# Hybrid FoX/mLSTM/PEER block on one core: the second token block's key searches spread among its own products, and one staging buffer for the first half of the gate table

## The chip, the core and the metric

One Trainium2 chip, one of its cores. The program runs once per execution; the metric is the device time of that execution in microseconds (us). TensorE is called PE, VectorE DVE, ScalarE ACT, GpSimd POOL and SyncE SP, as in the profile. DVE, ACT, PE, POOL and SP each work through a queue of their own in order; a wait at the head of a queue holds back all that stands behind it there.

## The reference, cut to what matters

The layer is a mixer (attention and mLSTM heads) followed by PEER, a lookup in a table of 16384 one-neuron experts. The change lies in PEER alone:

```python
q = (h @ w_query).reshape(B, S, PEER_HEADS, PEER_QDIM)      # 256 tokens, 8 heads x 256
s1 = einsum('bshd,nd->bshn', q[..., :half], sub_keys_1)     # 128 keys
s2 = einsum('bshd,nd->bshn', q[..., half:], sub_keys_2)
v1, i1 = top_k(s1, 16);  v2, i2 = top_k(s2, 16)
cand = (v1[..., :, None] + v2[..., None, :])                # 256 sums
vs, pos = top_k(cand, 16)
idx = i1[pos // 16] * 128 + i2[pos % 16]                    # 16 experts of a head
g = softmax(vs)
a = gelu(einsum('td,thkd->thk', x, expert_down[idx]))       # 2048 wide
out = einsum('thk,thkd->td', g * a, expert_up[idx])
```

## The kernel before, in words

The 256 tokens are two blocks of 128 (`t` = 0, 1), one token to a partition. After the mixer, the PEER part has four pieces.

*Search.* `head(t, h)` finds the 16 experts of head h for block t: `keys` and `chosen` are some 35 small DVE instructions that read the scores from `later[t]` and write `idx[t]` (in the order below `idx_4976` is block 0, `idx_4977` block 1). 16 searches in all.

*Gather and products.* The rows of `expert_down` are fetched by indirect DMA on POOL's queue, one DMA for one expert slot k of all 128 tokens: 128 rows of 2048 floats, 1 MB, into a tile `rows`. `issue()` fetches as many as there are free buffers. The buffers are those of the tags in the list `homes`, two to a tag, taken in turn: eight with `raw`, `rawb`, `hi`, `lo`, six without `lo`. `dot()` takes the oldest one: a DVE instruction multiplies the tile by the token's `ht[t]` and sums into `dots[t]`; then its buffer is free. 128 products to a block. `ready` holds the slots that are found and not yet fetched, block 0 first; `waiting(t)` counts those of block t.

*Gates as a table.* When block t's searches are over, `softmax(t)` runs on DVE with an Exp on ACT in between (DVE's next step, the sum into `gs`, waits for it). When its 128 products are over, `turned(t, [2])` makes the weights. Then the weights are scattered into a table (one column for each expert) with PE: for 16 tokens at a time, `first_ones(tb)` builds 16 one-hot matrices `o1` and `gates(tb)` the weighted `o2`, PE multiplies them, `out_of_psum()` copies the results on ACT to the tile `stage` (12 of 16 column groups) and to `kept` (the other 4), in four pieces of 4 tokens; after the fourth, SP sends `stage` to DRAM (`gd<-stage`, 768 KB, in pieces of 512 bytes). `tb` 0 to 7 are the first half of the table (block 0; `o1` and `o2` built on ACT), 8 to 15 the second (`o2` on DVE). `out_of_psum` runs behind: the last two pieces of `tb` are copied after the first `o2` of `gates(tb + 1)`.

*Up projection.* `expert_up` is multiplied by the table on PE (the long last stage), with the last 512 columns done by a second gather, `rows<-in_upr`.

Before, the order written out by hand is: six of block 0's searches alternate with three of block 1's, 14 to 16 products of block 0 between; then block 0's softmax and its last 26 products; then block 1's searches 4 to 7, four products after each, `gates(0)` in between; `softmax(1)`; then 112 products, and with them `gates(1)` to `gates(7)`. `later[0]`, `later[1]`, `stage` and the loaded `g` share the tag `q`, which has two buffers in turn. All the instructions of this part are issued through one helper, so their line in the profile is L69.

Of the kernel before, what the change touches and what calls it, by code (L numbers as in the profile page):

```python
# [7 lines left out]
F32 = mybir.dt.float32  # L8
# [10 lines left out]
P = 128  # L19
D = 2048  # L20
KD = D // P
T = 256
NT = T // P
# [10 lines left out]
PEER_H = 8  # L34
# [46 lines left out]
def hybrid_block(ctx: ExitStack, tc: tile.TileContext, x, c, wada, cst, shp, wst, wg, wmv, wfv,  # L81
# [485 lines left out]
    todo = {i: [] for i in range(24)}  # L567
# [28 lines left out]
    for b in range(KD):  # L596
        o = gemm_p(wout[b], lambda k: cath[k // 8][:, k % 8], lambda k: catl[k // 8][:, k % 8])
        g = mod[:, GATE1 * KD + b:GATE1 * KD + b + 1]
# [61 lines left out]
    pg = ctx.enter_context(tc.tile_pool(name="pg", bufs=2))  # L660
# [42 lines left out]

    slots = pk.tile([P, TOPK], BF16, bufs=1, name="slots")
    nc.scalar.activation(slots, iota[:, 0:TOPK], AF.Copy)
    later = [pg.tile([P, PEER_H, 2, P], F32, tag="q", name="later") for _ in range(NT)]
    sp = [None]

    def query(u):
# [50 lines left out]
    ready, flight = [], []  # L760
# [14 lines left out]
    def dot(n=1):  # L775

        for _ in range(n):
            if not flight:
                return
            _, t, k, u = flight.pop(0)  # L780
            nc.vector.scalar_tensor_tensor(u, u, 1.0, ht[t], op0=ALU.mult, op1=ALU.mult,
                                           accum_out=dots[t][:, k:k + 1])
            issue()

    def softmax(t):
        g = ev[t][:, 2]
        nc.vector.tensor_tensor(g, vs[t], vs[t][:, :, 0:1].to_broadcast([P, PEER_H, TOPK]), op=ALU.subtract)
        nc.scalar.activation(g, g, AF.Exp)
        gs = pk.tile([P, PEER_H], F32, tag="gs", name="gs")
        nc.vector.reduce_sum(gs, g, axis=AX.X)  # L790
        nc.vector.reciprocal(gs, gs)
        nc.vector.tensor_tensor(g, g, gs[:, :, None].to_broadcast([P, PEER_H, TOPK]), op=ALU.mult)

    def turned(t, parts):

        if 2 in parts:
            w = flat(ev[t][:, 2], 0, PEER_H)
            nc.scalar.activation(dots[t], dots[t], AF.Gelu)
            nc.vector.tensor_tensor(w, w, dots[t], op=ALU.mult)
        ep = bank([P, len(parts), P], "at")  # L800
        for i, p in enumerate(parts):
            nc.tensor.transpose(ep[:, i], flat(ev[t][:, p], 0, PEER_H), ident)
        nc.scalar.activation(est[t][:, parts[0]:parts[-1] + 1], ep, AF.Copy)


    TB = 16
# [6 lines left out]
    def first_ones(tb, engine=None):  # L813

        half, t0 = divmod(tb * TB, P)
        if 2 * HB - 4 <= tb < 2 * HB - 2:
            o1 = px.tile([P, TB, P], F32, name="o1")
        else:
            o1 = (ring, pg)[tb % 2].tile([P, TB, P], F32, tag=("lo", "o1")[tb % 2], name="o1", bufs=2)
        if engine is None:  # L820
            for tl in range(TB):
                t = t0 + tl
                nc.scalar.activation(o1[:, tl], iota, AF.Abs, bias=est[half][:, 0, t:t + 1], scale=-1.0)
            nc.scalar.activation(o1, o1, AF.Relu, scale=-1.0, bias=one)
        else:
            engine.tensor_tensor(o1, iota[:, None, :].to_broadcast([P, TB, P]),
                                 est[half][:, 0, t0:t0 + TB, None].to_broadcast([P, TB, P]), op=ALU.is_equal)
        ones_at[tb] = o1

    def gates(tb):  # L830
        if not kept:
            kept.append(const.tile([P, GK, T, 8], F32, tag="hs", name="kept"))
        stage = pg.tile([P, 16 - GK, TB, 8], F32, tag="q", name="stage")
        ts = slice(tb * TB, (tb + 1) * TB)
        half, t0 = divmod(tb * TB, P)
        col = est[half]
        o1 = ones_at.pop(tb)
        for t8 in range(0, TB, 8):

            o2 = pg.tile([P, 8, P], F32, tag="o2", name="o2")  # L840
            for tl in range(8):
                t = t0 + t8 + tl
                if half:
                    nc.vector.tensor_scalar(o2[:, tl], iota, col[:, 1, t:t + 1], col[:, 2, t:t + 1],
                                            op0=ALU.is_equal, op1=ALU.mult)
                else:
                    nc.scalar.activation(o2[:, tl], iota, AF.Abs, bias=col[:, 1, t:t + 1], scale=-1.0)
            if not half:
                nc.scalar.activation(o2, o2, AF.Relu, scale=-1.0, bias=one)
                for tl in range(8):  # L850
                    t = t0 + t8 + tl
                    nc.scalar.activation(o2[:, tl], o2[:, tl], AF.Copy, scale=col[:, 2, t:t + 1])
                out_of_psum()
            for t4 in range(0, 8, 4):
                gp = bank([P, 4, P], "at")
                for i in range(4):
                    nc.tensor.matmul(gp[:, i], o1[:, t8 + t4 + i], o2[:, t4 + i], start=True, stop=True)
                full.append((gp, stage, tb, t8 + t4))
            if half:
                out_of_psum()  # L860
# [14 lines left out]
    def head_scores(h):  # L875
        qs = [query(2 * h)]
        qs.append(query(2 * h + 1))
        scores(2 * h, qs[0])
        if h == 0:
            for j in range(4):  # L880
                by_tokens(0, j)
        scores(2 * h + 1, qs[1])

    def head(t, h):
        keys(h, t, later[t][:, h])
        chosen(t, h, h + 1)
        issue()

    def waiting(t):
        return sum(r[0] == t for r in ready)  # L890

    head_scores(0)
    head(0, 0)
    head_scores(1)
# [3 lines left out]
    for j in range(4):  # L898
        by_tokens(1, j)
    head_scores(3)  # L900
    behind = [(0, 1), (0, 2), (1, 1), (0, 3), (0, 4), (1, 2), (0, 5), (0, 6), (1, 3), (0, 7)]
    for i, (t, h) in enumerate(behind):
        while t == 0 and waiting(0) > 2:
            dot()
        head(t, h)
        if i < 2:
            head_scores(4 + 2 * i)
            head_scores(5 + 2 * i)
        if i == 1:
            homes[:] = ["raw", "rawb", "hi", "lo"]  # L910
    softmax(0)
    turned(0, [0, 1])
    while flight[0][1] == 0:
        dot()
        if sum(f[1] == 0 for f in flight) + waiting(0) == 8:
            homes[:] = ["raw", "rawb", "hi"]
    turned(0, [2])
    for tb in (0, 1):
        first_ones(tb)
    head(1, 4)  # L920
    dot(4)
    gates(0)
    first_ones(2)
    head(1, 5)
    dot(4)
    first_ones(3)
    for h in (6, 7):
        head(1, h)
        dot(4)
    softmax(1)  # L930
    turned(1, [0, 1])
    pk_cm.__exit__(None, None, None)
    px_cm = tc.tile_pool(name="px", bufs=2)
    px = px_cm.__enter__()
    todo = len(flight) + len(ready) - 12
    for tb in range(1, HB):
        dot(todo // (HB - 1))
        gates(tb)
        first_ones(tb + 3)
    out_of_psum()  # L940
    for tb in range(HB + 3, HB + 6):
        first_ones(tb)


# [74 lines left out]

    def group(g):  # L1020
        if GK <= g < 16:
            gt[g] = pg.tile([P, T, 8], F32, tag="q", name="g")
            nc.sync.dma_start(gt[g], gd[g])

    def gated(b):
# [149 lines left out]
```

## Time and profile before

| | |
|---|---|
| time, median of 3 (lowest to highest) | 1948.27 us (1943.56 to 1955.91) |
| the profiled execution | 1948.02 us; span from the first to the last instruction 1946.3 us |
| busy, share of the span | PE 65%, DVE 87%, ACT 42%, POOL 45% |
| mean DMA rate | 341 GB/s |

The profiled execution stands 0.25 us under the median. The page gives the busy time of each engine over the whole span; the program has stages with different limits, so the shares of single stretches are what is read below. A dot's busy time on DVE reads 2.29 us, but dots that follow each other without a wait start 2.21 us apart: neighbours overlap by some 0.08 us, and a wait reads that much too short.

### The profile page before, as it was taken

The page shows a single profiled execution, that of the slowest core. Times are in us where ns is not written, and L with a number is a line of the kernel's source. Part 1 is how long each engine was busy: PE and PEld are TensorE (multiplying, and loading weights), DVE is VectorE, ACT ScalarE, POOL GpSimd, SP SyncE. Part 2 cuts the span into 40 slices and gives each one's busy share as a digit, 9 for nine tenths or more (in the row PEclk, how much of TensorE's full clock was granted, in tenths as well). Part 3 has the DMA queues.
Part 4 walks back from the last instruction along what each step waited for, and adds up shares of the span by engine and source line. Part 5 has one row for each costly group of instructions (what it writes and reads, how often), then busy time and mean ns, then how long its engine had stood idle before and what let it go on. Part 6 is the DMA issues. An engine that isn't in the chain of part 4 may idle for free. (4 is left out here: it accounts for less than half of the span.)

```text
span 1946.3 us, 24456 instructions
## 1 busy us (share of the span) xinstructions
PE 1271.7 (65%) x9078; PEld 1191.5 (61%) x9078; DVE 1685.3 (87%) x2383; ACT 813.5 (42%) x1324; POOL 869.7 (45%) x516
## 2 busy tenths in 40 slices
PE   5899999999999900000011322102699999999998
PEld 3899977798988700000011222102699999999998
DVE  7887898897787799999999888888788898888885
ACT  4332374584421000000074776801555555555552
POOL 0000000000004366666755888883167777677760
PEclk9999999999999955555555555555799999999999
DMA  9977767787869979797977999998699999999992
GB/s 396 369 317 289 286 258 294 290 335 285 314 238 422 420 293 421 318 382 320 371 305 282 421 421 421 421 423 352 194 369 354 347 386 371 375 372 386 364 359 100
DMA packets 126649, 663.71 MB, mean 341 GB/s; under 512 B 13377, under 2 KB 38337, under 8 KB 55745
## 3 DMA queue, kind: packets, MB, share of 16 engines
q1 hardware_dynamic: 69186, 326.58, 43.9%
q0 software_dynamic: 57344, 335.58, 42.6%
q8 instruction: 71, 1.16, 0.2%
q14 instruction: 48, 0.39, 0.0%
HBM read 647.42 MB, written 14.68 MB: 340 GB/s over the span
## 5 line engine op out<-in xcount | busy, mean ns | idle before, releaser
L69 POOL DMA_INDIRECT rows<-in_down,idx x256 | 513.9, 2007 | 822.8 <-DVE tk L69 582.4
L69 DVE SCALAR_TENSOR_TENSOR rows<-rows,ht 128x2048 f32<-128x2048 f32 x256 | 577.6, 2290 | 60.0 <-DMA rows<-in_down,idx 58.7
L69 POOL DMA_INDIRECT rows<-in_upr,idx x256 | 355.6, 1389 | 202.3 <-DVE acc L69 87.0
L69 PE MATMUL ps<-w,whi 128*128 128x256 f32 x2048 | 353.9, 278 | 9.5 <-ACT w L69 8.8
L69 PEld LDWEIGHTS ps<-w,whi 128*128 128x128 f32 x2048 | 310.8, 189 | 10.0 <-ACT w L69 9.0
L69 PE MATMUL at<-sh,e 128*128 128x128 f32 x6 | 2.2, 437 | 452.0 <-DVE e L69 452.0
L69 PE MATMUL ps<-w,wlo 128*128 128x256 f32 x1024 | 284.1, 277 | 0.0
L69 PEld LDWEIGHTS at<-sh,e 128*128 128x128 f32 x6 | 0.9, 197 | 453.0 <-issue 453.0
L69 PE MATMUL at<-o,o 128*128 128x128 f32 x512 | 95.7, 368 | 161.6 <-ACT o L69 153.2
L69 PEld LDWEIGHTS ps<-w,wlo 128*128 128x128 f32 x1024 | 193.4, 189 | 0.0
L69 PEld LDWEIGHTS at<-o,o 128*128 128x128 f32 x512 | 90.3, 272 | 167.3 <-ACT o L69 157.9
L69 DVE SCALAR_TENSOR_TENSOR acc<-rows,e,acc 128x512 f32<-128x512 f32 x254 | 189.4, 746 | 1.6
L69 PE MATMUL at<-w,wht 128*128 128x256 f32 x1536 | 189.5, 283 | 0.0
L69 PEld LDWEIGHTS at<-w,wht 128*128 128x128 f32 x1536 | 186.4, 192 | 0.0
L69 DVE TENSOR_TENSOR wlo<-raw,whi 128x1024 fp32r<-128x1024 f32 x128 | 155.6, 1219 | 25.0 <-ACT whi L69 20.0
L69 ACT ACTIVATE whi<-raw 128x1024 fp32r<-128x1024 f32 x128 | 128.6, 1053 | 116.2 <-PE ps L69 71.0
L113 ACT ACTIVATE whi<-raw 128x2048 fp32r<-128x2048 f32 x65 | 124.1, 1911 | 117.6 <-PE ps L347 28.1
L114 DVE TENSOR_TENSOR wlo<-raw,whi 128x2048 fp32r<-128x2048 f32 x65 | 148.4, 2286 | 24.9 <-ACT whi L113 24.7
L69 PE MATMUL ps<-hf,raw 128*128 128x256 f32 x512 | 115.1, 385 | 6.5 <-DMA raw<-in_wq 5.4
L69 ACT ACTIVATE wht<-raw 128x1024 fp32r<-128x1024 f32 x64 | 64.4, 1054 | 116.0 <-PE at L69 104.8
L69 ACT ACTIVATE e<-e 128x128 f32<-128x128 f32 x2 | 0.6, 309 | 267.8 <-DVE e L69 267.8
L69 PEld LDWEIGHTS ps<-hf,raw 128*128 128x128 f32 x512 | 97.3, 192 | 22.4 <-DMA raw<-in_wq 8.1
(248 smaller groups left out, 2858.4 us busy)
## 6 DMA issues: line engine op xcount, KB each, us to landing
raw<-in_up SPq DMA_DIRECT2D x96, 1024.0 KB
raw<-in_wada SPq DMA_DIRECT2D x45, 1024.0 KB
early<-in_wada SPq DMA_DIRECT2D x44, 1024.0 KB
raw<-in_wst SPq DMA_DIRECT2D x32, 1024.0 KB
raw<-in_wout SPq DMA_DIRECT2D x16, 1024.0 KB
raw<-in_wq SPq DMA_DIRECT2D x16, 1024.0 KB
gd<-stage SPq DMA_DIRECT2D x16, 768.0 KB
g<-gd SPq DMA_DIRECT2D x12, 1024.0 KB
```

Source lines behind the costliest of these rows:

```text
L69: return self.tc.keep_in_program_order(f(*args, **kwargs))
L113: nc.scalar.activation(hi, raw, AF.Copy)
L114: nc.vector.tensor_tensor(lo, raw, hi.bitcast(F32), op=ALU.subtract)
```

## The change

Block 1's searches no longer stand between block 0's. All of block 0's searches come first, then each of block 1's is placed as soon as at most 8 of block 1's found slots are still unfetched. A new function, `first_half`, is called after each product: once block 0's last product is done, it issues the whole first half of the table (`gates(0)` to `gates(7)`) in one go. `later[1]` stays in use longer, so the tag `q` is split into `q0` and `q1` with one buffer each, and the first half's `stage` uses `q0` alone. The second half's `stage` and the loaded `g` alternate between the two.

```diff
-    later = [pg.tile([P, PEER_H, 2, P], F32, tag="q", name="later") for _ in range(NT)]
+    later = [pg.tile([P, PEER_H, 2, P], F32, tag=f"q{t}", name="later", bufs=1) for t in range(NT)]
...
-        stage = pg.tile([P, 16 - GK, TB, 8], F32, tag="q", name="stage")
+        stage = pg.tile([P, 16 - GK, TB, 8], F32, tag=f"q{tb % 2 if tb >= HB else 0}", name="stage", bufs=1)
...
+    halves = [-1]
+
+    def first_half():
+
+        of_first = sum(f[1] == 0 for f in flight) + waiting(0)
+        if halves[0] == 0 and of_first == 8:
+            homes[:] = ["raw", "rawb", "hi"]
+            halves[0] = 1
+        if halves[0] == 1 and of_first == 0:
+            halves[0] = 2
+            turned(0, [2])
+            for tb in range(4):
+                first_ones(tb)
+            for tb in range(HB):
+                gates(tb)
+                if tb + 4 < HB:
+                    first_ones(tb + 4)
+            out_of_psum()
...
-    behind = [(0, 1), (0, 2), (1, 1), (0, 3), (0, 4), (1, 2), (0, 5), (0, 6), (1, 3), (0, 7)]
+    behind = [(t, h) for t in range(NT) for h in range(1, PEER_H)]
     for i, (t, h) in enumerate(behind):
-        while t == 0 and waiting(0) > 2:
+        while waiting(t) > (2, 8)[t] or (t and waiting(0)):
             dot()
+            first_half()
         head(t, h)
...
-    while flight[0][1] == 0:
-        dot()
-        if sum(f[1] == 0 for f in flight) + waiting(0) == 8:
-            homes[:] = ["raw", "rawb", "hi"]
-    turned(0, [2])
-    for tb in (0, 1):
-        first_ones(tb)
-    head(1, 4)
-    dot(4)
-    gates(0)
-    first_ones(2)
...
+        if (t, h) == (0, PEER_H - 1):
+            halves[0] = 0
+            softmax(0)
+            turned(0, [0, 1])
     softmax(1)
     turned(1, [0, 1])
...
-    todo = len(flight) + len(ready) - 12
-    for tb in range(1, HB):
-        dot(todo // (HB - 1))
-        gates(tb)
-        first_ones(tb + 3)
-    out_of_psum()
-    for tb in range(HB + 3, HB + 6):
+    for tb in range(HB, HB + 6):
         first_ones(tb)
...
-            gt[g] = pg.tile([P, T, 8], F32, tag="q", name="g")
+            gt[g] = pg.tile([P, T, 8], F32, tag=f"q{g % 2}", name="g", bufs=1)
```

On DVE, at the first of the three places where a search of block 1 stood between block 0's: the end of that search, and the products behind it.

```order
-L69 TENSOR_TENSOR lk<-ab,slots 128x512
-L69 TENSOR_TENSOR lk<-lk,ki_4963 128x512
-L69 TENSOR_REDUCE e_4975<-lk 128x2x16
-L69 SCALAR_TENSOR_TENSOR idx_4977<-e_4975 128x16
 L69 SCALAR_TENSOR_TENSOR rows,dots_4978<-rows,ht_4960 128x2048 x14
 L69 MAX kv<-later 128x8
```

The 14 products (`dots_4978` is block 0's) now follow straight on block 0's search (0, 2); the searches (1, 1), (1, 2) and (1, 3) have gone from here.

On DVE, behind the search (1, 4) of before, the end of a search of block 1 and the products up to the next one.

```order
 L69 TENSOR_REDUCE e_4975<-lk 128x2x16
 L69 SCALAR_TENSOR_TENSOR idx_4977<-e_4975 128x16
-L69 SCALAR_TENSOR_TENSOR rows,dots_4979<-rows,ht_4961 128x2048 x4
+L69 SCALAR_TENSOR_TENSOR rows,dots_4979<-rows,ht_4961 128x2048 x16
 L69 MAX kv<-later 128x8
```

Where 4 products of block 1 (`dots_4979`) stood between two searches, there are 16. In full, DVE's order behind the search (0, 2) is now 14 products, then four times a search with 16 products, search (0, 7) with softmax(0) and 26 products, 2 products of block 1, six times a search with 16 products, the search (1, 7), softmax(1), 30 products. Before, 112 products stood behind softmax(1).

On ACT, at the Exp of softmax(1) (`e_4975`), in the kernel before: it stands between the `o1` of `tb` 3 and the first `o2` of `gates(1)`.

```order
L69 ACTIVATE o_6392<-sh,est_4972 128x128 x16
L69 ACTIVATE o_6392<-o_6392,one 128x2048
L69 ACT_TABLE_LOAD
L69 ACTIVATE e_4975<-e_4975 128x128
L69 ACTIVATE est_4973<-at 128x256
L69 ACTIVATE o_6557<-sh,est_4972 128x128 x8
```

The same place in the changed kernel.

```order
L69 ACTIVATE stage<-at 128x4x12x8
L69 ACTIVATE kept<-at 128x4x4x8
L69 ACT_TABLE_LOAD
L69 ACTIVATE e_4975<-e_4975 128x128
L69 ACTIVATE est_4973<-at 128x256
L69 ACTIVATE o_7299<-sh,est_4973 128x128 x16
```

The Exp has moved behind the last copy to `stage` of the first half, and the `o1` of `tb` 8 to 13 (six times 16 matrices) behind the Exp.

## Rows read from the trace of the kernel before

**Rows 1.** Engine busy by stretch: length, busy us (instructions) of each, PEclk, DMA share, GB/s

```profile
732.00:780.00 48.00, 0.00 (x0) 0.00 (x0) 47.07 (x88) 0.00 (x0) 30.39 (x16) 0.50 1.01 418
780.00:828.00 48.00, 0.00 (x0) 0.00 (x0) 47.07 (x80) 0.00 (x0) 30.40 (x16) 0.50 0.79 319
...
1068.00:1116.00 48.00, 15.93 (x69) 14.45 (x67) 41.39 (x37) 40.59 (x116) 42.52 (x19) 0.54 1.02 422
...
1452.00:1500.00 48.00, 48.00 (x418) 48.00 (x417) 43.02 (x48) 26.45 (x23) 34.92 (x26) 1.00 0.94 354
```

**Rows 2.** Groups of instructions from 684 to 1348 us: the products on DVE

```profile
L69 DVE SCALAR_TENSOR_TENSOR rows<-rows,ht 128x2048 f32<-128x2048 f32 x232 | 523.0, 2290 | 37.5 <-DMA rows<-in_down,idx 36.2 <-issue 0.9
```

**Rows 3.** DVE in order of time, searches (from their first MAX8) and products of block 0

```profile
673.54 0.29 DVE L69 MAX8 kv<-later 128x8 f32<-128x128 f32 x1
...
681.98 0.29 DVE L69 MAX8 kv<-later 128x8 f32<-128x128 f32 x1
...
706.05 2.29 DVE L69 SCALAR_TENSOR_TENSOR rows<-rows,ht 128x2048 f32<-128x2048 f32 x1
...
723.63 0.29 DVE L69 MAX8 kv<-later 128x8 f32<-128x128 f32 x1
...
732.20 2.29 DVE L69 SCALAR_TENSOR_TENSOR rows<-rows,ht 128x2048 f32<-128x2048 f32 x1
...
767.60 0.29 DVE L69 MAX8 kv<-later 128x8 f32<-128x128 f32 x1
...
981.15 2.28 DVE L69 SCALAR_TENSOR_TENSOR rows<-rows,ht 128x2048 f32<-128x2048 f32 x1
```

**Rows 4.** DVE in order of time, softmax(1) and products of block 1

```profile
1053.18 0.29 DVE L69 TENSOR_TENSOR e<-vs 128x128 f32<-128x128 f32 x1
...
1054.61 2.28 DVE L69 SCALAR_TENSOR_TENSOR rows<-rows,ht 128x2048 f32<-128x2048 f32 x1
...
1094.57 2.29 DVE L69 SCALAR_TENSOR_TENSOR rows<-rows,ht 128x2048 f32<-128x2048 f32 x1 [0.36 <-DMA rows<-in_down,idx]
...
1097.23 2.29 DVE L69 SCALAR_TENSOR_TENSOR rows<-rows,ht 128x2048 f32<-128x2048 f32 x1 [0.36 <-DMA rows<-in_down,idx]
...
1296.73 2.29 DVE L69 SCALAR_TENSOR_TENSOR rows<-rows,ht 128x2048 f32<-128x2048 f32 x1 [0.21 <-DMA rows<-in_down,idx]
...
1299.20 2.29 DVE L69 SCALAR_TENSOR_TENSOR rows<-rows,ht 128x2048 f32<-128x2048 f32 x1 [0.17 <-DMA rows<-in_down,idx]
...
1345.19 2.29 DVE L69 SCALAR_TENSOR_TENSOR rows<-rows,ht 128x2048 f32<-128x2048 f32 x1 [1.41 <-DMA rows<-in_down,idx]
```

**Rows 5.** POOL in order of time, the first gather after a pause

```profile
695.19 2.75 POOL L69 DMA_INDIRECT rows<-in_down,idx  x1 [20.36 <-DVE rows L69]
```

**Rows 6.** ACT in order of time, building the first half of the table

```profile
984.91 4.76 ACT L69 ACTIVATE o<-sh,est 128x128 f32<-128x128 f32 x16
...
1061.04 2.44 ACT L69 ACTIVATE o<-sh,est 128x128 f32<-128x128 f32 x8
...
1067.04 0.47 ACT L69 ACTIVATE stage<-at 128x384 f32<-128x384 f32 x1
...
1068.10 4.78 ACT L69 ACTIVATE o<-sh,est 128x128 f32<-128x128 f32 x16
...
1074.82 2.43 ACT L69 ACTIVATE o<-sh,est 128x128 f32<-128x128 f32 x8
...
1092.85 0.49 ACT L69 ACTIVATE stage<-at 128x384 f32<-128x384 f32 x1 [4.88 <-DMA gd<-stage]
...
1121.54 0.49 ACT L69 ACTIVATE stage<-at 128x384 f32<-128x384 f32 x1 [7.75 <-DMA gd<-stage]
```

**Rows 7.** SP in order of time: the writes of the first and of the second half

```profile
1061.01 184.56 SPq L69 DMA_DIRECT2D gd<-stage  x8
...
1356.21 43.37 SPq L69 DMA_DIRECT2D gd<-stage  x8
```

**Rows 8.** ACT in order of time: `gates(10)`'s first copy to `stage`

```profile
1361.70 0.49 ACT L69 ACTIVATE stage<-at 128x384 f32<-128x384 f32 x1 [1.77 <-PE at L69]
```

More of the change, by code (lines that the diff above doesn't have):

```diff
@@ L910, in hybrid_block @@
             homes[:] = ["raw", "rawb", "hi", "lo"]
-    softmax(0)
-    turned(0, [0, 1])
-    while flight[0][1] == 0:
-        dot()
-        if sum(f[1] == 0 for f in flight) + waiting(0) == 8:
-            homes[:] = ["raw", "rawb", "hi"]
-    turned(0, [2])
-    for tb in (0, 1):
-        first_ones(tb)
-    head(1, 4)
-    dot(4)
-    gates(0)
-    first_ones(2)
[L924 to L929, printed above, removed]
+        if (t, h) == (0, PEER_H - 1):
+            halves[0] = 0
+            softmax(0)
+            turned(0, [0, 1])
     softmax(1)
```

## The prediction

> **What bounds the kernel now.** I read the busy time by stretch first, because the change lies in one stage, from about 670 to 1348 us. Up to 1068 us DVE is the limit: 47.07 of 48 us busy, while the share of the DMA engines swings between 1.01 (one search between products) and 0.79 (two searches in a row, or searches with few products) [rows 1]. From 1068 us it is the other way: DMA at 1.02, DVE at 41.4 of 48. In the last stage PE is full (48.00 of 48) and nothing there is touched, so what the gather stage gains or loses arrives at the end one for one, less what the passage between the stages eats; that passage (second half of the table, DVE's and PE's) keeps its order.
>
> So both resources take turns at waiting. The products waited 37.5 us in all by the list of groups [rows 2]. Second view: DVE in order of time, which gives prices. A search takes 681.98 - 673.54 = 8.44 us; 16 products without a wait take 767.60 - 732.20 = 35.40, 2.2125 each [rows 3]. A softmax with Exp ready takes 1.43 [rows 4].
>
> **The most that it can bring.** No instruction goes. Both orders agree until the search at 673.54. From there 13 searches (109.7), 232 products (513.3) and two softmaxes (2.9) make 625.9, with 0.7 for a step between the blocks 626.6; without any wait the last product would end at 1300.1. It ends at 1345.19 + 2.21 = 1347.4 [rows 4]. The difference is 47.3: the 37.5 listed, plus 0.08 for each of some 127 waits that the overlap of neighbours hides. 47 us is the ceiling; four kinds of waits take their part of it back.
>
> **First term, block 0: 2.2 us.** Before, 14 products after the searches (0, 2) and (1, 1) ran from 690.42 to 723.63 [rows 3], 33.2 instead of 31.0. They start with six buffers in both versions, so I keep the 2.2. The cycles behind it have one search, 16 products and eight buffers: 43.8 us on DVE, against 16 gathers at 2.47 (1296.73 to 1299.20, [rows 4]) = 39.5 on DMA. Precisely such a stretch stands at 732.20 to 767.60, with DMA at 1.01 and not one wait [rows 1, 3]. So block 0's last product ends three searches earlier, at 983.4 - 25.3 = 958.0.
>
> **Second term, block 1's cycles: 5 us (0 to 18).** Here there are six buffers. After a pause the eighth product started at 706.05, 0.15 later than DVE alone would have (690.42 + 7 x 2.2125); its gather was the second that POOL issued after 695.19, the first followed the second product's end (694.9) by 0.3 [rows 3, 5]. With 2.47 between landings the first landed at 703.6: 8.7 us from a free buffer to a landed tile. After a search the seventh product needs the first one's buffer: 2.3 + 8.7 = 11.0 against 13.3 on DVE, and the sixteenth 11.0 + 9 x 2.47 = 33.2, against 33.2: even. While a table write is under way gathers land 2.66 apart (1094.57 to 1097.23, [rows 4]), and the sixteenth is 1.7 late. About 0.9 a cycle, six cycles of 44.7. The low end is no wait at all; the high end, 3 us a cycle, is a return later than 8.7 by one more landing (2.47), since the 8.7 rests on one place.
>
> Block 1's first search ends at 958.0 + 0.7 + two products + 8.44 = 971.6, and six cycles on DVE reaches softmax(1) at 1240.
>
> **Third term, the wait at softmax(1): 12 us (0 to 26).** This is the new wait. The Exp now stands on ACT behind the whole first half of the table. DVE's sum waits for it, and behind that sum stand 30 products. What ACT has to do: the first `o1` starts 1.5 us after the last product of block 0 (984.91 against 983.4), at 959.5. An `o1` costs 6.72 (1068.10 to 1074.82), half a `gates` 6.0 of building and 1.06 of copying (1061.04, 1067.04, 1068.10) [rows 6]. Four `o1`, `gates(0)`, one more `o1` with up to 3 us for PE to leave its buffer, and the first half of `gates(1)`: the first write goes out at 1016.
>
> Then each `gates` needs the one buffer, so each write must land before the next is filled. How long is a write? The copies that waited for one are 28.7 apart (1092.85, 1121.54), with 7.75 us idle of ACT ahead of the second, and even the first wait, at 1092.85, ended over 31 us after the first write's issue at 1061.01 [rows 6, 7]. Eight times 28.7 from 1062 ends at 1292, and that is where the products' step falls from 2.66 to 2.47 [rows 4]; so beside a full gather queue a write lasts about 31 us, alone or in a row. When gathers pause it is quick: the write issued at 1356.21 had left its buffer by 1361.70 [rows 7, 8]. With a second buffer the 28.7 would hide behind ACT's work, with one it does not.
>
> The Trainium skill's page "Trainium Kernel Development and Optimization", section Best Practices, asks for double buffers so that DMA overlaps compute; the change does the opposite here, and by that rule this third term is its price.
>
> DMA pauses once in each cycle. The last six gathers land by 33.2 + 6 x 2.5 = 48, 4 us after the next search's end, their engines done a little earlier, and the next gather cannot move before the first product is over, POOL has run its 2.75 us [rows 5] and a little more: some 3 us from the search's end +3 to +6. Search ends: 1016, 1061, 1106, 1150, 1195, 1240. Write 0 (1016) meets the pause at 1019 and lands at 1022. ACT's work between landing and next write is 1.06 + 6.72 + 7.06 = 14.8 while an `o1` is left, 8.1 later. Write 1 goes at 1037 and lands in the pause, 1066; write 2 1081 to 1111; write 3 1126 to 1156; write 4 1164 to 1195; write 5 1203, just past the pause, to 1234; write 6 at 1242. By then DVE has stood at softmax(1) for 2 us, the gathers run dry, and it lands at about 1249. Four pairs of copies less the two already done (2.1) and the Exp (1.4 allowed, a whole softmax [rows 4]) end at 1252.5, where DVE alone would have had it at 1240.7.
>
> **Fourth term, the last 30 products: 6 us (4 to 10).** By the second term's rule product 30 starts at 11.0 + 23 x 2.47 = 67.8 after the restart, against 64.2, and the last write slows eleven gathers by 0.19: 5.7. The six `o1` behind the Exp take 40 us on ACT and are hidden under these 72; the second half of the table finds them ready.
>
> **Sum.** 47.3 - 2.2 - 5 - 12 - 5.7 = 22 us. From the profiled execution's 1948.0 that gives 1926, and the median shown stands 0.25 us higher: 1926. The four ends together reach from 39 us gained to 8.
>
> **Rivals.**
>
> *Quick writes, no wait at softmax(1): 1908 to 1915.* If a write passes a busy gather in 20 us or less, ACT is through at about 1016 + 3 x 35 + 3 x 28 + 24 = 1229, before DVE arrives. The gain is then 47.3 - 2.2 - 5 - 5.7 = 34 us, and up to 39 if the cycles lose less as well. For it: DMA is 5% less loaded than in the stretch that shows 28.7. Against it: the first write, alone and partly before the queue was full, took 31 as well [rows 6, 7]. The Trainium skill ("DMA: Bandwidth & Descriptors", section Queues, rings and completion order) has each DMA engine go round its queues by whole packets, typically 9 to 17 descriptors. By that rule the 96 pieces of a write on each engine would be through in some ten turns, about 4 us; the trace's 28.7 is nearer to one piece for each gathered row (some 90 rows pass in that time), so here the measurement decides.
>
> *The writes meet no pause: 1935 to 1942.* With 31 us for each, write 5 goes at 1232; DVE stops at 1240, writes 5 and 6 finish in the quiet, the Exp comes at 1266. The wait is 26, the gain 8: 1940. For it: with a write under way the pause may close. Against it: six buffers run out by arithmetic.
>
> *Gathers return later than 8.7 us: 1931 to 1936.* Each cycle loses 2 us more, but softmax(1) comes later by the same 12, and its wait shrinks to some 3; the last 30 lose 4 more. Gain 15.
>
> *Slower: 1979.* The write is slow by itself, not because gathers share its engines: then the standing DVE does not speed writes 5 and 6, they end at 1263 and 1302, the Exp comes at 1306, the wait is 65 us and the loss 31. It turns to a loss from an Exp at about 1275 on. Against it stands the write of 5.5 us in the passage [rows 7, 8].
>
> *It does nothing.* If block 1's late searches only shift idle time back to DMA, with gathers never ahead, about 1940 to 1950. Against it: the two limits are separated in time now, 0.79 of DMA there and 41 of 48 of DVE here [rows 1].
>
> **How the numbers follow.** Forecast (1919 to 1931) 0.43; quick writes 0.23; no pause 0.14; late gathers 0.10; slower 0.05; nothing 0.05. About 1% (19.5 us, to 1928.8) is what a measurement of this kernel tells from no change. Three quarters of the forecast and all of quick writes lie below: faster 0.58. Slower by over 1% is its own case, 0.05; the rest, 0.37, lies within 1%. Range 1908 to 1941: it leaves out the slower case, most of doing nothing and the tail of quick writes.
>
> **What would show it.** DVE: (1, 1), (1, 2), (1, 3) gone from block 0; that block's last product near 958; search ends of block 1 about 44.7 apart; one long idle time of about 12 us before `gs` of softmax(1), near 1240; the last product near 1325. ACT: waits for `gd<-stage` before almost every `gates`, 25 to 30 us, and none or short at the first. DMA share near 0.95 from 960 to 1240, with dips after each search. If the wait before `gs` is missing, or over 30 us, the third term was wrong; if search ends stand 47 apart, the second.

## The result, and the profile after

The changed kernel takes 1929.17 us (median of six runs, 1924.65 to 1936.38), the kernel before 1948.8 in its six runs (1943.56 to 1955.91). The ratio is 0.9897 with a 95% interval of 0.9874 to 0.992: 19.6 us faster, 1.0% (0.8 to 1.3), with no run of the one among those of the other. 1926 was predicted, with a range of 1908 to 1941. The profiled execution took 1930.43 us, its span 1928.7.

The places where a time is read, DVE in order of time in the changed kernel: the search (0, 2) and the ends of its 14 products, block 0's last product, the first product behind block 1's searches (1, 1) and (1, 2), then softmax(1), the product behind it and the last one.

```profile
671.93 0.29 DVE L69 MAX8 kv<-later 128x8 f32<-128x128 f32 x1
...
680.36 2.28 DVE L69 SCALAR_TENSOR_TENSOR rows<-rows,ht 128x2048 f32<-128x2048 f32 x1
...
713.28 0.29 DVE L69 MAX8 kv<-later 128x8 f32<-128x128 f32 x1
...
953.88 2.28 DVE L69 SCALAR_TENSOR_TENSOR rows<-rows,ht 128x2048 f32<-128x2048 f32 x1
...
969.62 2.28 DVE L69 SCALAR_TENSOR_TENSOR rows<-rows,ht 128x2048 f32<-128x2048 f32 x1
...
1014.37 2.28 DVE L69 SCALAR_TENSOR_TENSOR rows<-rows,ht 128x2048 f32<-128x2048 f32 x1
...
1243.17 0.28 DVE L69 TENSOR_TENSOR e<-vs 128x128 f32<-128x128 f32 x1
1258.85 0.29 DVE L69 TENSOR_REDUCE gs<-e 128x8 f32<-128x128 f32 x1 [15.39 <-ACT e L69]
...
1259.61 2.29 DVE L69 SCALAR_TENSOR_TENSOR rows<-rows,ht 128x2048 f32<-128x2048 f32 x1
...
1329.29 2.29 DVE L69 SCALAR_TENSOR_TENSOR rows<-rows,ht 128x2048 f32<-128x2048 f32 x1 [1.42 <-DMA rows<-in_down,idx]
```

From the search's start at 671.93 to the last product's end at 1331.5 it is 659.6 us; before, from 673.54 to 1347.4, it was 673.9 [rows 3, 4]. DVE's own work in it is 626.6 in both, so its waits fell from 47.3 to 33.0: 14.3 us gained in the stage. The stage also began 1.6 us earlier, which lies ahead of the change, and the way from the last product to the end took 597.2 instead of 598.9. Together these are the 17.6 us between the spans.

The 33.0 us fall on the prediction's four terms so (a cycle is 16 products and the search of block 1 behind them, 43.84 us on DVE without a wait):

| | predicted | measured | how it is read |
|---|---|---|---|
| block 0, 14 products | 2.2 | 1.9 | 713.28 - 680.36 = 32.9 against 31.0 |
| block 1, six cycles | 5 | 10.5 | 1243.17 - 969.62 = 273.5 against 6 x 43.84 |
| wait at softmax(1) | 12 | 15.4 | the wait before `gs` |
| last 30 products | 5.7 | 5.5 | 1331.5 - 1259.61 = 71.9 against 66.4 |

They sum to 33.3; the 0.3 too many is the 0.38 us that the sum into `gs` waits even with the Exp ready (as at softmax(0)), which DVE's own 626.6 already holds.

Now the groups of instructions from 684 to 1345 us in the changed kernel, then its list of waits there (us in total, times, longest).

```profile
L69 DVE SCALAR_TENSOR_TENSOR rows<-rows,ht 128x2048 f32<-128x2048 f32 x231 | 515.7, 2286 | 14.1 <-DMA rows<-in_down,idx 13.2 <-issue 0.4
```

```profile
ACT stage L69 <- DMA gd<-stage: 131.3, 6, 27.9
...
DVE gs L69 <- ACT e L69: 15.8, 2, 15.4
DVE rows L69 <- DMA rows<-in_down,idx: 13.2, 39, 1.9
```

The idle time ahead of products has fallen from 37.5 us to 14.1 [rows 2], and in its place stands one wait of 15.4. ACT waits 131.3 us in six waits for the table's buffer. Its rows show them one by one, with the Exp at their end.

```profile
1020.72 0.49 ACT L69 ACTIVATE stage<-at 128x384 f32<-128x384 f32 x1 [2.85 <-DMA gd<-stage]
...
1065.18 0.49 ACT L69 ACTIVATE stage<-at 128x384 f32<-128x384 f32 x1 [23.50 <-DMA gd<-stage]
...
1111.48 0.49 ACT L69 ACTIVATE stage<-at 128x384 f32<-128x384 f32 x1 [25.35 <-DMA gd<-stage]
...
1156.73 0.49 ACT L69 ACTIVATE stage<-at 128x384 f32<-128x384 f32 x1 [24.29 <-DMA gd<-stage]
...
1198.34 0.49 ACT L69 ACTIVATE stage<-at 128x384 f32<-128x384 f32 x1 [27.37 <-DMA gd<-stage]
...
1240.48 0.49 ACT L69 ACTIVATE stage<-at 128x384 f32<-128x384 f32 x1 [27.90 <-DMA gd<-stage]
...
1258.51 0.31 ACT L69 ACTIVATE e<-e 128x128 f32<-128x128 f32 x1
```

Each of these starts is the landing of a write: 1020.7, 1065.2, 1111.5, 1156.7, 1198.3, 1240.5. Predicted were 1022, 1066, 1111, 1156, 1195, 1234.

Busy time by stretch, the first three as in [rows 1] and then the one with the wait in it:

```profile
732.00:780.00 48.00, 0.00 (x0) 0.00 (x0) 47.38 (x71) 0.00 (x0) 34.07 (x18) 0.50 0.97 395
780.00:828.00 48.00, 0.00 (x0) 0.00 (x0) 47.38 (x71) 0.00 (x0) 34.12 (x18) 0.50 0.94 379
1068.00:1116.00 48.00, 7.38 (x32) 6.93 (x32) 44.83 (x69) 22.49 (x66) 29.98 (x17) 0.57 0.95 378
1212.00:1260.00 48.00, 10.13 (x46) 9.25 (x44) 29.82 (x59) 19.70 (x58) 21.83 (x11) 0.54 0.83 329
```

The swing of DMA between 1.01 and 0.79 in block 0 has become an even 0.97 and 0.94, with DVE full. In block 1 DVE rose from 41.4 to 44.8 of 48. The fourth stretch, with DVE at 29.8, is where part of this is given back.

### The profile page after: what moved, and what is told of

Read it like the earlier page. It is cut to its first block, busy times and chain, and to the rows that moved or that the text cites. A ratio compares the mean times of both kernels' runs of the same rounds, so it can differ in the third digit from the quotient of the medians.

```text
span 1928.7 us, 24437 instructions
## 1 busy us (share of the span) xinstructions
PE 1269.6 (66%) x9078; PEld 1189.8 (62%) x9078; DVE 1678.6 (87%) x2383; ACT 813.8 (42%) x1324; POOL 832.9 (43%) x516
## 5 line engine op out<-in xcount | busy, mean ns | idle before, releaser
L69 POOL DMA_INDIRECT rows<-in_down,idx x256 | 477.6, 1866 | 843.2 <-DMA raw<-in_wq 579.6
L69 ACT ACTIVATE o<-sh,est 128x128 f32<-128x128 f32 x352 | 105.9, 393 | 0.4 <-PE at L69 0.4
```

The costliest lines, as they stand in the source:

```text
L69: return self.tc.keep_in_program_order(f(*args, **kwargs))
```

## The experiments

The main theory: block 1's spread searches bring the gain; one staging buffer takes some 15 us of it back through the Exp; the six cycles lose to a DMA pause and its return. The rivals: the wait at softmax(1) is only shifted idle time, and would come back in the products if removed; a table write is long by its size and not by the gathers beside it; the cycles lose to the writes alone.

**Two staging buffers.** The changed kernel, with the first half's `stage` taken in turn from `q0` and from `ht0`, which is free by then.

```diff
-        stage = pg.tile([P, 16 - GK, TB, 8], F32, tag=f"q{tb % 2 if tb >= HB else 0}", name="stage", bufs=1)
+        stage = pg.tile([P, 16 - GK, TB, 8], F32, tag=f"q{tb % 2}" if tb >= HB else ("q0", "ht0")[tb % 2],
+                        name="stage", bufs=1)
```

> The changed kernel, but the first half's staging tiles alternate between q0 and the tile ht0, which block 0's products no longer need. Theory (the wait of 15.4 us before the sum of softmax(1) is the one staging buffer: each write of about 30 us must land before ACT goes on): ACT fills the next buffer while a write is under way, the Exp is ready before DVE comes, the wait falls to about 0.4 us. The searches' ends in block 1 stay 45 to 46 apart, the last product ends 13 to 16 us earlier than in the changed kernel, near 1316, and the time is 1913 to 1918 us. Rival (ACT's own work is too long for the place of the Exp, whatever the buffers): the wait stays above 8 us and the time above 1921 us.

Measured: 1915.22 us (1914.47 to 1917.95), ratio to before 0.9825 (0.9803 to 0.9846). The list of waits from 684 to 1345 us:

```profile
ACT stage L69 <- DMA gd<-stage: 29.5, 3, 14.6
...
DVE rows L69 <- DMA rows<-in_down,idx: 13.1, 45, 1.4
...
DVE gs L69 <- ACT e L69: 0.8, 2, 0.4
```

The wait at softmax(1) is gone (0.4), the products' waits are as before (13.1 against 13.2), and the six cycles take 273.3 us against 273.5. So the 15 us were not idle time that had to fall somewhere; they were the price of the one buffer in this order, and nothing else was late in their place.

**No writes of the first half.** What do the cycles lose without any write beside the gathers?

```diff
-            if to == TB - 4:
+            if to == TB - 4 and tb >= HB:
...
-            nc.sync.dma_start(gt[g], gd[g])
+            for i in range(NT):
+                nc.sync.dma_start(gt[g][:, i * P:(i + 1) * P], gd[g, :, P:])
```

> The changed kernel without the eight writes of the table's first half (12 of 16 column groups of block 0; the last stage reads block 1's part twice in their place, so the output lacks block 0's part of these groups). It parts the two causes of block 1's cycles being 45.6 us long (273.5 us for six) instead of 43.8. Theory A (the writes slow the gathers, 2.66 against 2.48 us a gather, and with six buffers that shows at the end of each cycle): cycles of 43.9 to 44.3, six in 263 to 266 us, no wait at softmax(1), last product near 1304, time 1900 to 1906 us. Theory B (six buffers are too few by themselves, a gather returns too late after a search): cycles stay at 45 us or more, six in 270 us or more, last product at 1311 or later.

Measured: 1912.35 us in one run. The first product behind the search (1, 1) and the start of softmax(1) on DVE:

```profile
969.75 2.29 DVE L69 SCALAR_TENSOR_TENSOR rows<-rows,ht 128x2048 f32<-128x2048 f32 x1
...
1238.49 0.28 DVE L69 TENSOR_TENSOR e<-vs 128x128 f32<-128x128 f32 x1
```

The six cycles take 268.7 us: 5.7 over DVE's 263.0, where the changed kernel has 10.5. They fell between the two expectations; writes account for 4.8, something else for 5.7. What that is, the stretches behind one search of this kernel show. The search ends at 1103.5, and the cycle that follows loses the most of the six, 2.1 us (columns as in [rows 1]: the last two are the DMA share and GB/s).

```profile
1106.00:1108.00 2.00, 0.00 (x0) 0.00 (x0) 2.00 (x3) 1.97 (x7) 1.98 (x1) 0.50 0.08 33
1108.00:1110.00 2.00, 0.74 (x3) 0.74 (x4) 2.00 (x1) 1.97 (x6) 1.70 (x2) 0.50 0.41 66
1110.00:1112.00 2.00, 2.00 (x12) 2.00 (x11) 2.00 (x3) 2.00 (x8) 1.70 (x2) 0.50 0.76 291
1112.00:1114.00 2.00, 1.05 (x5) 0.75 (x4) 2.00 (x3) 2.00 (x9) 1.70 (x2) 0.50 0.98 393
1114.00:1116.00 2.00, 0.00 (x0) 0.00 (x0) 2.00 (x3) 1.94 (x5) 1.70 (x2) 0.50 1.07 320
1116.00:1118.00 2.00, 1.68 (x8) 1.68 (x9) 2.00 (x3) 2.00 (x8) 1.70 (x2) 0.50 0.86 311
1118.00:1120.00 2.00, 2.00 (x10) 1.81 (x9) 2.00 (x3) 2.00 (x9) 1.83 (x1) 0.50 1.00 414
```

The pause that the prediction worked out is there, some 3 us with 33 and 66 GB/s. But full speed (414 GB/s) is reached only at 1118: in the eight microseconds between it is 291 to 393. The other five cycles come back likewise, with slices of 274 to 430 GB/s before a steady 401 and more. The prediction let gathers land 2.47 us apart from the first on.

**Only four searches spread, twice.** What is it worth that (1, 1), (1, 2) and (1, 3) leave block 0 as well? The kernel with two buffers, with these three put back between block 0's searches.

```diff
-    behind = [(t, h) for t in range(NT) for h in range(1, PEER_H)]
+    behind = [(0, 1), (0, 2), (1, 1), (0, 3), (0, 4), (1, 2), (0, 5), (0, 6), (1, 3), (0, 7),
+              (1, 4), (1, 5), (1, 6), (1, 7)]
...
-        while waiting(t) > (2, 8)[t] or (t and waiting(0)):
+        while (t == 0 and waiting(0) > 2) or (h > 3 and (waiting(1) > 8 or waiting(0))):
```

> Two staging buffers as in the run above, but the order of before in block 0: (1, 1), (1, 2) and (1, 3) stand between its products again; only (1, 4) to (1, 7) are spread, one for 16 of block 1's products. Theory (what counts is DVE work moved out of the stretch where DVE is the limit into the stretch where DMA is; each search counts): about 52 products of block 1 run with no search between them at 2.66 us, so some 20 us of waiting stay, the last product ends 17 to 23 us later than with all seven spread, and the time is 1930 to 1940 us. Rival (it is enough that no long run of searches with four products each leaves DMA idle; the three early searches cost nothing where they were): within 5 us of the run with all seven spread.

Measured: 1965.46 us (1964.15 to 1974.98), ratio 1.01 (1.0067 to 1.0133), a miss. The condition `h > 3` holds for block 0's own late searches too, so that these waited for block 1's products. The first half of the table began only at 1116 on ACT, and DVE waited 53.1 us before `gs` at 1290.3, although two buffers left ACT only a 2.2 us wait for a write. It is no test of the question, but it shows the same Exp from another side: here the first half starts late, and DVE waits for ACT's own work on it, some 170 us, with hardly a wait for a buffer in it. The mended kernel:

```diff
+        while waiting(0) > 2 if t == 0 else h > 3 and (waiting(1) > 8 or waiting(0)):
```

> The order meant in the run with four spread searches: two staging buffers, (1, 1) to (1, 3) between block 0's products as before, then 26 and 50 products without a search, then (1, 4) to (1, 7) with 16 products after each. Theory (each search moved from the stretch that DVE limits into the one that DMA limits counts): block 0's last product ends 25 us later than with all seven moved, near 981; the 50 products run 2.5 to 2.7 us apart; the wait at softmax(1) stays under 1 us; the last product ends near 1336 and the time is 1930 to 1937 us, 15 to 22 us above the run with two buffers and all seven moved. Rival (spreading the last four is enough): 1913 to 1920 us.

Measured: 1934.65 us (1930.8 to 1943.31), ratio 0.9913 (0.9879 to 0.9947). No wait at softmax(1), but block 0's last product ends at about 982 again, and the products wait 24.8 us in 80 waits. The search (0, 2) and the step behind the last product on DVE, here and then with all seven searches spread and the same two buffers:

```profile
672.34 0.29 DVE L69 MAX8 kv<-later 128x8 f32<-128x128 f32 x1
...
1332.06 0.29 DVE L69 TENSOR_TENSOR e<-e,dots 128x128 f32<-128x128 f32 x1 [0.38 <-ACT dots L69]
```

```profile
672.89 0.29 DVE L69 MAX8 kv<-later 128x8 f32<-128x128 f32 x1
...
1318.60 0.29 DVE L69 TENSOR_TENSOR e<-e,dots 128x128 f32<-128x128 f32 x1 [0.38 <-ACT dots L69]
```

It is 659.7 us here and 645.7 there. Moving the three out of block 0 is thus worth 14.0 us in the gather stage. The medians differ by 19; what the other 5 are stays open, since the one profile is of the slowest of the four runs (1943.31), with a last stage of 545 us (the last section).

**One staging buffer in the old order.** The kernel before, with only the tags of the change.

```diff
-        stage = pg.tile([P, 16 - GK, TB, 8], F32, tag="q", name="stage")
+        stage = pg.tile([P, 16 - GK, TB, 8], F32, tag=f"q{tb % 2 if tb >= HB else 0}", name="stage", bufs=1)
...
```

> The kernel before with the other half of the change alone: q0 and q1 with one buffer each, the first half's staging in q0 only, the order of searches and table as before. Theory (a write beside a full gather queue lasts 29 to 31 us and nothing overlaps it with one buffer): ACT's period for 16 tokens grows from 28.7 to 45 to 46 us, the first half's last write is not out before 1345, the six o1 tiles and the gelu of block 1 stand behind it on ACT, and the passage to the last stage begins 20 to 40 us late: 1968 to 1990 us. Rival (the staging buffer has slack, the cost was only the place of the Exp): within 5 us of the kernel before.

Measured: 1983.73 us (1970.45 to 1988.18), ratio 1.0158 (1.0112 to 1.0204). Two of ACT's six waits in order of time, and after that DVE behind its last product:

```profile
1093.82 0.49 ACT L69 ACTIVATE stage<-at 128x384 f32<-128x384 f32 x1 [27.71 <-DMA gd<-stage]
...
1334.07 0.49 ACT L69 ACTIVATE stage<-at 128x384 f32<-128x384 f32 x1 [27.40 <-DMA gd<-stage]
```

```profile
1339.04 2.29 DVE L69 SCALAR_TENSOR_TENSOR rows<-rows,ht 128x2048 f32<-128x2048 f32 x1 [0.18 <-DMA rows<-in_down,idx]
...
1385.61 0.29 DVE L69 TENSOR_TENSOR e<-e,dots 128x128 f32<-128x128 f32 x1 [44.27 <-ACT dots L69]
```

The buffer alone costs some 34 us by the medians (22 to 40 by the interval). The products end no later than before, but ACT reaches block 1's gelu (`dots`) only at 1385, and DVE stands for 44 us behind the products instead of ahead of 30 of them. The two halves of the change taken apart are thus -34 us (the order, with two buffers) and +34 (one buffer in the old order); together they are -20. Why the buffer costs less in the new order was not tried apart. The rows show two things that work that way: the first write goes out 48 us earlier (SP issues it at 1011.7 there, at 1060.0 here), and while DVE stands at softmax(1) and the gathers stop, a write takes at most 6 us.

**Long pieces.** Is a write long because it has 1536 pieces of 512 bytes that take turns with gathered rows? The changed kernel, one buffer, with the table in DRAM laid out so that a write is 128 pieces of 6 KB; the loads of `g` then read in 512-byte pieces instead.

```diff
-    gd = dram.tile([16, P, T, 8], F32, name="gd")
+    gd = dram.tile([2 * HB, P, 16 - GK, TB, 8], F32, name="gd")
...
-                nc.sync.dma_start(gd[GK:, :, tb * TB:(tb + 1) * TB, :].rearrange("g p t e -> p g t e"), stage)
+                nc.sync.dma_start(gd[tb], stage)
...
```

> The changed kernel with its one staging buffer, but the table lies in DRAM so that a write is 128 pieces of 6 KB instead of 1536 of 512 bytes (the loads of g in the last stage then read pieces of 512 bytes). Theory (a write is long beside gathers because each of its pieces waits its turn with gathered rows, not because of its bytes): the waits of ACT for a write fall from 23 to 28 us to under 6, the Exp of softmax(1) is ready before DVE comes, the last product ends 13 to 17 us earlier than in the changed kernel and the time is 1911 to 1918 us, as with two buffers. Rival (the length comes from the bytes, or from the latency of the queue): waits of 20 us and more, the wait before the sum of softmax(1) above 8 us, 1924 us and more.

Measured: 1919.28 us (1918.12 to 1922.32), ratio 0.9839 (0.9809 to 0.9869). The waits from 684 to 1345 us:

```profile
ACT stage L69 <- DMA gd<-stage: 19.9, 7, 3.2
DVE rows L69 <- DMA rows<-in_down,idx: 15.3, 39, 1.7
...
DVE gs L69 <- ACT e L69: 0.8, 2, 0.4
```

Same bytes, same single buffer, same gathers beside them, and ACT's longest wait falls from 27.9 to 3.2 us. So the many short pieces made the write long, not its size and not the gathers' load by itself. The six cycles are no better (275.7). The time is a little over what was expected; in the profile (1922.32 us) the last stage took some 6 us longer (the last section below).

**Both.** Long pieces and two staging buffers.

> Long pieces and two staging buffers together. Theory: both take away the same wait, so nothing is added: within 3 us of either alone, 1911 to 1918 us. Rival (each takes away a part): below 1909 us.

Measured: 1920.92 us (1917.62 to 1925.34), ratio 0.9849 (0.9814 to 0.9884). From block 0's end to block 1's, 363.2 us against 362.7 with long pieces alone: both take away the same wait, and the second adds nothing. The time is within 2 us of long pieces alone, but 5.7 over two buffers alone, where 3 was expected: the six cycles take 276.3 us here, 3 more than with short pieces.

**A seventh gather buffer, twice.** If the cycles lose to the return after a pause, one more tile in store covers it. The kernel with long pieces does not need `ht0` for `stage`, so it becomes a seventh home in block 1.

```diff
...
+            homes[:] = ["raw", "rawb", "hi", "ht0"]
...
```

> Long pieces, one staging buffer, and the tile ht0 as a seventh buffer for gathers once block 0 is over (its search order shifts by one to three products). Theory (5.7 of the 10.5 us that block 1's six cycles lose, and the 5.5 of the last products, come from six buffers: after a search DMA pauses until the first product is over and needs some 8 us to come back to its full rate): cycles of 43.9 to 44.6 us, the last product 5 to 9 us earlier than with long pieces alone, 1904 to 1910 us. Rival (DMA's rate, not the buffers, sets these ends): within 3 us of long pieces alone.

Measured: 1963.26 us (1955.76 to 1971.05), ratio 1.0069 (1.0046 to 1.0092), a miss. `issue` goes round the list and stops where a home is full; a home with one buffer in every fourth place stops the round until its one gather is used up. Cycles of 16 products took 49.8 to 54.6 us, and the products waited 49.8 us in 60 waits from 950 to 1345. Without intent this is the price of fewer gathers under way. With the list in the right proportion:

```diff
+            homes[:] = ["raw", "rawb", "hi", "raw", "rawb", "hi", "ht0"]
```

> Long pieces, one staging buffer and a seventh gather buffer, now taken once in a round of seven (before, its turn came every fourth gather, and with one buffer that let only some four gathers be under way). Theory (part of what block 1's cycles and the last products lose comes from six buffers, which run out while DVE searches): cycles of 43.9 to 45.0 us where long pieces alone had 44.5 to 48.7, the last product 4 to 9 us earlier after block 0's end than with long pieces alone (362.7 us), and the time 1910 to 1916 us. Rival (DMA's rate over a cycle, with the writes, is the limit, and a buffer more only shifts the wait): within 3 us of long pieces alone.

Measured: 1913.9 us (1912.11 to 1914.53), ratio 0.9827 (0.9798 to 0.9857). The last products of block 0 and block 1, here and then with long pieces alone:

```profile
954.49 2.28 DVE L69 SCALAR_TENSOR_TENSOR rows<-rows,ht 128x2048 f32<-128x2048 f32 x1
...
1310.42 2.29 DVE L69 SCALAR_TENSOR_TENSOR rows<-rows,ht 128x2048 f32<-128x2048 f32 x1 [1.42 <-DMA rows<-in_down,idx]
```

```profile
951.19 2.28 DVE L69 SCALAR_TENSOR_TENSOR rows<-rows,ht 128x2048 f32<-128x2048 f32 x1
...
1313.91 2.29 DVE L69 SCALAR_TENSOR_TENSOR rows<-rows,ht 128x2048 f32<-128x2048 f32 x1 [1.44 <-DMA rows<-in_down,idx]
```

Block 0's end to block 1's is 355.9 us instead of 362.7: one more buffer gives back 6.8 us, as the theory of the return wants it. 4.4 of it lie in the six cycles and 2.4 behind softmax(1). The cycles themselves, 267.0 us and 275.7, are no fair pair: the shifted order leaves the first of them 14 products, so that they lose 8.3 us here and 12.7 there.

**Searches cut in three.** Better than to cover the pause is not to have it. The kernel with two staging buffers, with five products after each of a search's two sets of keys; the threshold goes from 8 to 18, since ten products now lie within the search.

```diff
...
+            yield
...
-    def head(t, h):
-        keys(h, t, later[t][:, h])
+    def head(t, h, between=0):
+        for _ in keys(h, t, later[t][:, h]):
+            for _ in range(between):
+                dot()
+                first_half()
...
-        while waiting(t) > (2, 8)[t] or (t and waiting(0)):
+        while waiting(t) > (2, 18)[t] or (t and waiting(0)):
...
-        head(t, h)
+        head(t, h, 5 * t)
```

> Two staging buffers, and each of block 1's searches cut in three parts with five products between the parts, so that DVE never leaves the gathers for more than some 4 us. Theory (the search of 8.4 us in one piece empties the six buffers; DMA pauses for some 3 us and comes back slowly, and that is what is lost at the end of each cycle): no pause of DMA in block 1, cycles of 43.8 to 44.6 us, six of them 263 to 268 us where two buffers alone had 273.3, the last product 5 to 10 us earlier, the time 1905 to 1911 us. Rival (DMA's rate is the limit): within 3 us of two buffers alone, 1912 to 1918 us.

Measured: 1910.46 us (1903.86 to 1918.21), ratio to before 0.9809 (0.978 to 0.9838). The ends of the searches (1, 1) and (1, 7) on DVE, and the sum of softmax(1):

```profile
970.94 0.17 DVE L69 SCALAR_TENSOR_TENSOR idx<-e 128x16 uint32<-128x16 f32 x1
...
1233.94 0.17 DVE L69 SCALAR_TENSOR_TENSOR idx<-e 128x16 uint32<-128x16 f32 x1
...
1234.69 0.29 DVE L69 TENSOR_REDUCE gs<-e 128x8 f32<-128x128 f32 x1 [0.38 <-ACT e L69]
```

Six cycles in 263.0 us: exactly DVE's own work, not a microsecond of waiting. DMA has no pause in them either: from 978 to 1234 no slice of 4 us falls under 312 GB/s. The stretch from 1068 to 1116 in this kernel:

```profile
1068.00:1116.00 48.00, 14.73 (x64) 13.55 (x64) 47.38 (x71) 37.50 (x109) 33.68 (x19) 0.57 1.02 417
```

DVE is full (47.38 of 48) and DMA is full (1.02, 417 GB/s) at once, with six gather buffers, with short pieces and with writes under way. This is the lowest median, 36 us under before's in the same comparison (1946.31), against 19.6 for the change as it came. Its runs spread over 14 us and overlap those of two buffers alone; clear of that is the gather stage, 10 us shorter than with two buffers alone. That the cut and the threshold came together was not taken apart; by the code, the old threshold would let the gathers run out of found slots within a search.

## Why the prediction was right, and where it was not

**The ceiling and the direction** held. Two limits that took turns were brought together in time, and 14.3 us of the 47.3 of waits are gone, by the profile; 19.6 us by the medians, of which the earlier start and the shorter way to the end lie outside the stage. The sum had 22 us gained in the stage, so the stage itself fell 8 us short. That the time is only 3 us off is in part luck: 3.3 us came from outside the stage and 2 from the spread of the runs, and no term forecast them.

**First and fourth term** held (1.9 for 2.2, 5.5 for 5.7). The fourth was right in size and not wholly in its parts: 2.1 of its 5.7 us were to come from the last write, but without any writes of the first half the 30 products still take 72.1 us. With seven buffers 31 products take 71.8, one more from store in the same time and so a loss of 3.2 us: behind the store there are 24 gathers in both. So it is the gathers' own pace there, and the last one's late landing (1.42 us).

**Second term: mis-sized, 5 us for 10.5.** The step that failed is "the sixteenth 11.0 + 9 x 2.47 = 33.2, against 33.2: even". It takes DMA at full rate as soon as the first gather has landed. Without writes a cycle still loses 0.95 us (5.7 in six), where that step has nothing; the writes' part, 0.8 a cycle, is what the step on the 2.66 had made it, 0.9. A seventh buffer takes away 4.4 us of the cycles' loss, and searches cut in three, without a pause, take away all of it. The slow return could have been read ahead: it stands in the kernel before, behind the one pause from which the prediction took its 8.7 us.

```profile
700.00:704.00 4.00, 0.00 (x0) 0.00 (x0) 4.00 (x5) 0.00 (x0) 3.39 (x3) 0.50 1.00 403
704.00:708.00 4.00, 0.00 (x0) 0.00 (x0) 3.93 (x3) 0.00 (x0) 3.39 (x3) 0.50 0.97 328
```

From 708 on it is 424. By an estimate from these rows, 8 us at a mean of 366 instead of 424 put the gathers back by 1.1 us, about what a cycle loses without writes. The range given for the term, 0 to 18, held it.

**Third term: right in its mechanism, 12 us for 15.4.** Two staging buffers or long pieces remove it whole, and the chain of landings was met to within 2 us up to write 3. Counted from ACT's fourth copy, the writes took 9, 30, 31, 30, 34, 34 and at most 6 us: the first met the pause and the last the quiet, as worked out, and writes 1 to 3 took the 31 that [rows 6, 7] gave. Writes 4 and 5 were 3 us longer than that, so write 5 landed at 1240.5 instead of 1234 and the Exp ended at 1258.8 instead of 1252.5; DVE, held up by the second term, was there 3 us later than worked out, and 3.4 us were left over.

**The rivals.** *Quick writes* fell: the writes took 30 to 34 us beside the gathers, as the rows of before had shown. Its price was sound: without the wait 1915.22 us was measured, where its range ended at 1915. 12 times longer pieces made the waits short, so a write's time goes by its pieces here; by the time, about one short piece passes for one gathered row, or ten for a whole gather's eight rows on an engine, which the runs do not part. The Trainium skill's rule in "DMA: Bandwidth & Descriptors", section Queues, rings and completion order, that engines go round their queues by whole packets of typically 9 to 17 descriptors, gave some 4 us a write in the prediction, and the trace differs from that figure. But the figure is an estimate that lets ten pieces of the write pass in a turn and only about one gathered row. If the gather's eight rows pass in one turn too, ten turns are ten gathers, 10 x 2.66 = 27 us by an estimate from the same rule, and that is near the trace. So the runs speak against the 4 us, and not against the rule. *No pause met* fell by the first write's 9 us, though only that one gained much by a pause. *Slower* fell with its mechanism: write 6, beside stopped gathers, took at most 6 us, so a write is not slow by itself. That the same buffer costs 34 us in the old order has another cause (the place of the gelu behind the writes), and its likeness to the rival's 31 is chance. *Gathers return late* was near: not the first landing but the rate behind it is late, 0.95 us a cycle where it gave 2 more; it names the cause of the second term's miss, though not the time. *It does nothing* fell by the 19.6 us.

**The sums.** They come out, but for two. The four ends of the terms, added up as they stand, reach from 41 us gained to 9 lost; 39 and 8 are the best case of *quick writes* and the case of *no pause met*. And three quarters of the forecast with all of quick writes make 0.55, not 0.58.

## What to carry to other kernels

Where two engines take turns as the limit, the searches or other small work of one stage belong between the bulk steps that wait for transfers, cut as fine as the buffers in flight can cover: a pause costs the transfers more than its length, since here they needed some 8 us to come back to their full rate. Before a buffer is taken away, look what stands behind its user in that engine's queue (here one Exp that another engine waits for), and count the pieces of the transfer that empties it. The halves of one change can have prices that depend on each other: here -34 and +34 us alone, -20 together. And where a rate behind a pause goes into a sum, read it behind the pause, not in the steady stretch.

## What the runs showed that was not expected

*The way back from a pause.* After some 3 us with the gather queue dry, the rate was 291, 393, 320 and 311 GB/s over the next 8 us before 414, with POOL busy issuing for 1.7 of every 2 us. The DMA share reads 0.76 to 1.07 in the same slices, so the engines are mostly busy while they move less. Whether this is the few gathers under way or the queue itself stays open; it was not tried apart.

*A write's length goes by its pieces.* 768 KB in 1536 pieces took 30 to 34 us beside gathers, the same bytes in 128 pieces kept ACT at most 3.2 us.

*The last stage is not always equally long.* From the first to the last matmul into `ps` it takes 532 us in nine of the twelve profiles, 538 to 539 in those of the kernels with long pieces alone and with cut searches, and 545 in that of the mended four searches. The matmuls of that stage, the changed kernel first and the kernel with cut searches after it (ns, lowest, median, highest; then the first and last start):

```profile
L69 PE MATMUL ps<-w,whi x2048: 275/276/580, 1385.1 to 1917.2; 128*128 128x256 f32 x187
```

```profile
L69 PE MATMUL ps<-w,whi x2048: 276/279/581, 1362.8 to 1901.3; 128*128 128x256 f32 x187
```

PE is full there in both, and the granted clock reads 1.00 from 1400 to 1900; the median matmul is 279 ns for 276, and 276 to 279 is as 532 to 538. With cut searches the stage runs like the other up to 1600 (868 matmuls in 100 us) and slower from there on (846 or 847 from 1700 to 1900, against 867 or 868). The kernel with long pieces and two staging buffers has 532.4, so it is not the layout of the table. The cause is open. It is why the profile with cut searches (1914.57 us) shows less than its gain in the gather stage, where it is 10 us ahead of the kernel with two buffers.
